# A hand-set order for the turn from the first FFN to the dilated attention

## The chip, the core and the metric

The kernel runs on one core of a Trainium2 chip. The metric is the device time of one execution in microseconds (us). Most of the work is fp32 matrix products on TensorE. Each fp32 operand is split into a high part and a low part, and a product is made of three matmuls: high by high, high by low, low by high.

## The reference

A block of two layers works on 512 tokens of 1024 features. Layer 0 has an HGRN2 mixer and a SwiGLU FFN, layer 1 a dilated attention of three groups and a second FFN. The change lies between the first FFN and the attention:

```python
def rms_norm(x, g):
    xf = x.astype(jnp.float32)
    y = xf * lax.rsqrt(jnp.mean(xf * xf, axis=-1, keepdims=True) + NORM_EPS)
    return (y * g.astype(jnp.float32)).astype(x.dtype)
...
    proj = (u @ w_in).astype(jnp.float32).reshape(B, S, N_GROUPS, 3, ATT_HEADS, ATT_HEAD_DIM)
    for gi, (window, dilation) in enumerate(DILATED_GROUPS):
        q = apply_partial_rope(proj[:, :, gi, 0], cos, sin) * scale
        k = apply_partial_rope(proj[:, :, gi, 1], cos, sin)
        v = proj[:, :, gi, 2]
...
        y = swiglu_ffn(u, ffn_w_in[layer], ffn_w_out[layer])
        h = h + (1.0 + g2) * rms_norm(y, norm_g[layer, 3])
```

So the turn takes the FFN's output y, adds its normalized and gated form to h, normalizes the new h into u, and multiplies u by the attention's weights. The values of the first group (eight heads, 1024 columns) come first, in two halves of 512 columns.

## The kernel before

**Tiles.** The 512 tokens are four tiles of 128 (t = 0 to 3), the 1024 features eight tiles of 128 (kt = 0 to 7). uh and ul hold the high and the low part of u with the features on the partitions. A value product of one half for one token tile is 8 x 3 = 24 matmuls of 512 columns in one PSUM bank (`three`, L582 to L584), with weights in two tiles: kt 0 to 3 and kt 4 to 7.

**The turn, step by step** (class `Turn`, L603 on). For each token tile: squares of y (`sq_y`, ScalarE, L618), gating (`gated`, VectorE, L627), a reciprocal root (`r_y`, VectorE L631 and GpSimd L633), the update of h (`upd`, VectorE, L643), squares of h (`sq_h`, ScalarE), a root again (`r_h`), the normalized row xn (VectorE, L657), eight transposes on TensorE into two banks (`flip`, L663), scale and shift into u (`u_of`: four steps on ScalarE, L673, and four on VectorE, L675), the high parts (`hi_of`, ScalarE, L678) and the low parts (`lo_of`, GpSimd, L682).

**Weights.** A `Stream` loads weights in a fixed sequence through two raw buffers on the SP queue (L67 to L76). `process_to` splits a whole tile of 2048 columns: high part on ScalarE (L96), low part on VectorE (L97). `pieces` does the same in two halves that the caller places (L116, L117). There are three buffers of high and low parts: the fourth value tile needs the buffer of the first, which the first half's products of all token tiles must have read. The sequence here is: first half, kt 0 to 3 and 4 to 7; second half, kt 0 to 3 and 4 to 7; the first query-key tile; then quarters for the next query-key pair and half tiles for further values.

**What sets the order.** Inside `with tc.manual_schedule(engines=ORDERED)` each of TensorE, ScalarE, VectorE and GpSimd keeps the order of the program text. Outside, the framework's scheduler chooses the order; it may also put such instructions between those of a hand-set stretch. The end of the first FFN (L1126 to L1185) is hand-set. It holds the value products of the first half (`v_prod`, copied out at L1675) and, among them, the transposes of token tiles 2 and 3; a half split of the third weight tile and four DMAs that store h (L1183) come behind these.

Then follows, left to the scheduler: the rearranged copies of uh and ul called `apart` (eight each on ScalarE, L1700, and VectorE, L1701), the products of the second half with `tok_proj` (L1480, copied out at L1683, stored at L1685), `token_sums` (four sums, L875, and four differences, L876 to L879, on VectorE; then four high parts over uh, ScalarE L883, and four low parts over ul, VectorE L884), and the masks (GpSimd L1707 to L1712, VectorE L1713 to L1716).

**The plan.** The rest of the attention is placed by `Plan`, which gives every task an engine, a cost and a due time and writes out one hand-set order. It begins with the first query-key tile (48 matmuls with `apart`, L1822). Next is a query-key pair made with seven products instead of eight: its weights are split and summed at L1868 to L1894, and its products use the parts from `token_sums`. Behind it come value units, whose weights are split at L2002 and L2003 and summed at L2007.

Of the kernel before, what the change touches and what calls it, by code (L numbers as in the profile page):

```python
# [11 lines left out]
F32 = mybir.dt.float32  # L12
# [5 lines left out]
P = 128  # L18
S = 512
D = 1024  # L20
KT = D // P
NT = S // P
# [5 lines left out]
ORDERED = {mybir.EngineType.PE, mybir.EngineType.Activation, mybir.EngineType.DVE, mybir.EngineType.Pool}  # L28
# [9 lines left out]
SEEN = lambda t: t.rearrange("p (x n a) -> p x a n", a=2, n=P)  # L38
PLACED = lambda t: t.rearrange("p (x a n) -> p x a n", a=2, n=P)
# [259 lines left out]
def block_kernel(tc, x, c, positions, ada_w, ada_b, norm_g, hgrn_w_in, lower, hgrn_norm_g, hgrn_w_out,  # L299
                 attn_w_in, attn_w_out, ffn_w_in, ffn_w_out, inv_freq, out):  # L300
    nc = tc.nc
    act, dve, pool, pe = nc.scalar, nc.vector, nc.gpsimd, nc.tensor
    x2, out2 = x[0], out[0]
    V4 = lambda t: t.rearrange("p (a b) -> p a b", a=4)
    L4 = lambda a: a.rearrange("p (l r) -> p r l", r=4)
    R4 = lambda a: a.rearrange("p (r l) -> p l r", r=4)

    with ExitStack() as ctx:
# [7 lines left out]
        def bank(tag):  # L316
            uid[0] += 1
            return psum.tile([P, 512], F32, name=f"ps_{tag}{uid[0]}", tag=tag, bufs={"mm": 4, "a": 2, "b": 2}[tag])
# [19 lines left out]
        h = base.tile([P, NT, D], F32, name="h")  # L338
# [183 lines left out]
        def av(g, hf):  # L522
            return [wtok(AW, kq, (g * 3 + 2) * D + hf * 512) for kq in range(2)]
# [9 lines left out]
        def values(hf, gs):  # L533

            for g in gs:
                order.append(("v", g, hf))
                at.extend([("half", w[1]) for w in av(g, hf)])
# [29 lines left out]
        st = Stream(nc, wp, items, 2, 3)  # L567
# [5 lines left out]
        uh = base.tile([P, KT, S], F32R, name="uh")  # L573
        ul = base.tile([P, KT, S], F32R, name="ul")
# [5 lines left out]
        def three(ps, ah, al, bh, bl, start, stop, part=False):  # L580
            ps, bh, bl = LAID(ps), TAKE(bh), TAKE(bl)
            pe.matmul(ps, ah, bh, start=start, stop=False, skip_group_check=part)  # L582
            pe.matmul(ps, ah, bl, start=False, stop=False, skip_group_check=part)  # L583
            pe.matmul(ps, al, bh, start=False, stop=stop, skip_group_check=part)  # L584
# [436 lines left out]
        def ffn(l, first, close, nxt, side):  # L1021
            turns.close()
            close()
            with ExitStack() as fx:
# [4 lines left out]
                with ExitStack() as qx:  # L1029
# [6 lines left out]
                    for j in range(PLAIN[l]):  # L1036
                        if j == 0:
                            pss = first
                        else:
                            pss = []  # L1040
                            for i in range(2):
                                w = st.take()
# [33 lines left out]
                for j in range(NJ - 2):  # L1076
# [3 lines left out]
                    w = st.take()  # L1080
# [5 lines left out]
                ws = [st.take(), st.take(1)]  # L1086
# [39 lines left out]
                with tc.manual_schedule(engines=ORDERED):  # L1126
                    mm(0)
                    y_steps(0)
                    n.upds(0)
                    n.r_h(0)  # L1130
                    n.xn(0)
                    mm(1)
                    y_steps(1)
                    n.upds(1)
                    mm(2, (0, 1))
                    n.flip(0, [bank("mm"), bank("a")])
                    n.u_of(0, 0)
                    n.u_of(0, 1)
                    n.r_h(1)
                    n.parts_of(0, 0)  # L1140
                    n.xn(1)
                    n.parts_of(0, 1)
                    mm(3, (0, 1))
                    for hi_f, lo_f in st.pieces(2, True):
                        hi_f()
                        lo_f()
                    st.fill()
                    mm(2, (2, 3))
                    y_steps(2)
                    n.upds(2)  # L1150
                    n.flip(1, [bank("mm"), bank("b")])
                    n.u_of(1, 0)
                    n.u_of(1, 1)
                    n.r_h(2)
                    n.parts_of(1, 0)
                    n.parts_of(1, 1)
                    n.xn(2)
                    mm(3, (2, 3))
                    y_steps(3)
                    fx.close()  # L1160
                    v_prod = nxt[1]()
                    vw = [st.take(0), st.take(0)]
                    v_prod(vw, 0, range(8))
                    n.upds(3)
                    n.flip(2, [bank("mm"), bank("a")])
                    n.r_h(3)
                    n.u_of(2, 0)
                    n.u_of(2, 1)
                    n.parts_of(2, 0)
                    n.parts_of(2, 1)  # L1170
                    n.xn(3)
                    v_prod(vw, 1, range(8))
                    n.flip(3, [bank("mm"), bank("b")])
                    n.u_of(3, 0)
                    n.u_of(3, 1)
                    n.parts_of(3, 0)
                    n.parts_of(3, 1)
                    for hi_f, lo_f in st.pieces(2, True):
                        hi_f()
                        lo_f()  # L1180
                    st.fill()
                    for t in range(NT):
                        act.dma_start(h_away[t], h[:, t])  # L1183
                    v_prod(vw, 2, range(8))
                    v_prod(vw, 3, range(8))  # L1185
                turns.close()


# [288 lines left out]
        head = sc.tile([P, S], F32, name="head")  # L1477
        pool.memset(head, 0.0)

        def tok_proj(done):  # L1480

            ws = [st.take(), st.take(1)]
            for t in range(NT):
                ps = bank("mm")
                tok = slice(t * P, (t + 1) * P)
                for kt in range(KT):
                    whi, wlo = ws[kt // 4]
                    w = slice((kt % 4) * 512, (kt % 4 + 1) * 512)
                    three(ps, uh[:, kt, tok], ul[:, kt, tok], whi[:, w], wlo[:, w], kt == 0, kt == KT - 1)
                done(t, ps)  # L1490

        C16 = lambda a: a.rearrange("p (c t) -> p c t", t=32)
        B44 = lambda a: a.rearrange("p (b c t) -> p b c t", b=4, c=4)

# [117 lines left out]
        for p in range(4):  # L1612
            tiles = []
            whi, wlo = st.take()
            for k in range(2):
                ps = block(whi, wlo, k * P, 256)
# [6 lines left out]
            whi, wlo = st.take()  # L1623
            for k in range(2):
                ps = block(whi, wlo, k * P, 256)
# [4 lines left out]
                if k == 1:  # L1630
                    for i in range(2):
                        n = fl.n + i
# [17 lines left out]
        oT, V, store = [], [], []  # L1650
        scr = dpool.tile([NH, 2, S, 2], F32, name="scr")
        h_away = dpool.tile([NT, P, D], F32, name="h_away")
        back = lambda t: lambda: act.dma_start(h[:, t], h_away[t])
        heads = {}
        def open_attention():

            ctx.enter_context(hx)
            otp = hx.enter_context(tc.tile_pool(name="a_ot", bufs=1))
            oT.extend(heads_of(otp))
            store.append(otp)  # L1660
            hx.enter_context(cx)
            vp = cx.enter_context(tc.tile_pool(name="a_v", bufs=1))
            V.extend(vp.tile([P, NT, 512], F32, name=f"V{g}") for g in range(3))
            banks = {}

            def v_prod(ws, t, kts):
                if t not in banks:
                    banks[t] = bank("mm")
                tok = slice(t * P, (t + 1) * P)
                for kt in kts:  # L1670
                    w = slice((kt % 4) * 512, (kt % 4 + 1) * 512)
                    three(banks[t], uh[:, kt, tok], ul[:, kt, tok], ws[kt // 4][0][:, w], ws[kt // 4][1][:, w],
                          kt == 0, kt == KT - 1)
                if kts[-1] == KT - 1:
                    act.copy(PLACED(V[0][:, t]), SEEN(banks[t]))  # L1675
            return v_prod

        ffn(0, first, h0.close, ((1, 0), open_attention), "right")
        v_away = dpool.tile([P, NT, 512], F32, name="v_away")

        def to_away(t, ps):

            act.copy(PLACED(V[1][:, t]), SEEN(ps))  # L1683
            if t == NT - 1:
                act.dma_start(v_away, V[1])  # L1685

        PNs, PR_h = [h[:, k].rearrange("p (t n) -> p t n", t=4) for k in range(2)], h[:, 2].rearrange("p (t n) -> p t n", t=4)
        flip_no = [0, 0]
# [7 lines left out]
        up = upx.enter_context(tc.tile_pool(name="a_u", bufs=1))  # L1696
        up.tile([P, 64], F32, name="pad")
        apart = [up.tile([P, KT, S], F32R, name=f"apart{k}") for k in range(2)]
        for kt in range(KT):
            act.copy(V4(apart[0][:, kt]), L4(uh[:, kt]).bitcast(F32))  # L1700
            dve.tensor_copy(V4(apart[1][:, kt]), L4(ul[:, kt]).bitcast(F32))  # L1701
        tok_proj(to_away)
        th, tl = (t.rearrange("p (a b) n -> p a (b n)", a=4).rearrange("p a (b n) -> p a b n", b=4) for t in (uh, ul))

        token_sums(th, tl, h.rearrange("p t (a n) -> p (t a) n", a=2), *apart)()
# [8 lines left out]
        dve.tensor_copy(lqf, lq)  # L1714
        dve.tensor_scalar(lqf, lqf, 0.5, NEG, op0=OP.is_ge, op1=OP.mult)
        dve.tensor_tensor(maskR[:, P:256], maskR[:, 0:P], lqf, op=OP.min)  # L1716

        plan = Plan()
        ticks, clock = Fillers(), [0.0]
# [534 lines left out]
        rows_of, ws, opened = [], [], ("opened", 0)  # L2254
# [104 lines left out]
```

## Time and profile before

| | us |
|---|---|
| median of three runs | 1475.56 |
| lowest and highest | 1474.87, 1476.01 |
| profiled execution | 1476.0 |
| its span in the trace | 1474.1 |
| TensorE, VectorE, ScalarE, GpSimd busy | 1430.7, 1113.8, 824.7, 190.1 |

The stretch that the change touches runs from about 650 to 702 us of the span. In a time line each row is: start, duration, engine, line, operation, out<-in, shapes, count. In square brackets stands the idle time of the engine before it and what ended that. PE is TensorE, DVE VectorE, ACT ScalarE, POOL GpSimd. SPq and ACTq are the queues that issue DMAs. A row with a count holds several instructions in a row, and its duration is theirs together.

### The profile page before, as it was taken

The numbers are of one execution on the slowest core, as the hardware profiler recorded it, in microseconds if no ns is written. First come the engines' busy times: TensorE is split into PE (matmuls) and PEld (weight loads), VectorE is DVE, ScalarE is ACT, GpSimd is POOL, SyncE is SP. The second block draws the span as 40 slices with busy tenths as digits, with TensorE's granted clock in tenths as the row PEclk, the third lists the DMA queues.
The fourth block names the chain that finished last, engine by engine and source line by source line (L and its number), as shares of the span: only waits on it lengthen the run. The fifth ranks groups of instructions, "written<-read, shape, count | busy, mean of one in ns | idle before, by whom it ended". The sixth has DMA issues, their size and how long they took to land. (4 is left out here: it accounts for less than half of the span.)

```text
span 1474.1 us, 25335 instructions
## 1 busy us (share of the span) xinstructions
PE 1430.7 (97%) x9903; PEld 1312.5 (89%) x9903; DVE 1113.8 (76%) x1800; ACT 824.7 (56%) x1484; POOL 190.1 (13%) x173
## 2 busy tenths in 40 slices
PE   8999999999999999998999999999999999999998
PEld 6777888889999987787998999999998999999887
DVE  4588688488888876777788877788776978887644
ACT  4434442474555542267748778657896645555332
POOL 1011102031111100231000110001012211110100
PEclk9999999999999999999999999999999999999999
DMA  9656554223333355734244543254344233334541
GB/s 308 192 192 197 172 173 145 84 78 94 110 109 111 108 178 195 230 113 143 90 122 119 147 123 109 64 172 137 94 138 149 86 104 112 110 110 149 191 143 58
DMA packets 212872, 201.10 MB, mean 136 GB/s; under 512 B 8920, under 2 KB 170640, under 8 KB 212496
## 3 DMA queue, kind: packets, MB, share of 16 engines
q1 hardware_dynamic: 209776, 192.71, 42.3%
q10 hardware_dynamic: 1952, 6.65, 1.2%
q8 instruction: 78, 1.28, 0.4%
q0 software_dynamic: 1024, 0.12, 0.2%
q14 instruction: 42, 0.34, 0.1%
HBM read 192.30 MB, written 5.30 MB: 134 GB/s over the span
## 5 line engine op out<-in xcount | busy, mean ns | idle before, releaser
L96 ACT CAST hi<-raw 128x2048 fp32r<-128x2048 f32 x41 | 78.1, 1904 | 140.7 <-DMA raw<-in_ffn_w_out_dram 82.5
L1822 PE MATMUL ps_mm<-apart,hiq 128*128 128x256 f32 (+1 forms) x608 | 137.4, 320 | 3.5 <-ACT xs L1936 2.8
L97 DVE TENSOR_TENSOR lo<-raw,hi 128x2048 fp32r<-128x2048 f32 x41 | 98.0, 2393 | 55.7 <-ACT hi L96 55.6
L582 PE MATMUL ps_mm<-uh,hi 128*128 128x512 f32 (+1 forms) x368 | 130.7, 355 | 0.0
L583 PE MATMUL ps_mm<-ul,hi 128*128 128x512 f32 (+1 forms) x368 | 128.4, 349 | 1.6 <-DVE ul L682 1.6
L584 PE MATMUL ps_mm<-uh,lo 128*128 128x512 f32 (+1 forms) x368 | 128.3, 349 | 0.0
L1822 PEld LDWEIGHTS ps_mm<-apart,hiq 128*128 128x128 f32 x608 | 99.9, 191 | 9.8 <-ACT xs L1936 3.4
L954 DVE TENSOR_TENSOR loq<-raw,hiq 128x1024 fp32r<-128x1024 f32 x72 | 85.0, 1221 | 20.2 <-ACT hiq L950 20.2
L963 PE MATMUL ps_mm<-th,hiq 128*128 128x256 f32 x360 | 99.0, 275 | 0.0
L963 PE MATMUL ps_mm<-tl,hiq 128*128 128x256 f32 x360 | 99.0, 275 | 0.0
L963 PE MATMUL ps_mm<-th,loq 128*128 128x256 f32 x360 | 99.0, 275 | 0.0
L1822 PE MATMUL ps_mm<-apart,loq 128*128 128x256 f32 (+1 forms) x304 | 95.4, 314 | 0.6 <-DVE loq L1958 0.6
L934 POOL TENSOR_TENSOR raw<-raw 128x512 f32<-128x512 f32 x36 | 47.7, 1326 | 320.1 <-DVE spare L930 165.3
L583 PE MATMUL ps_mm<-lo,oh 128*128 128x512 f32 x208 | 80.0, 385 | 5.5 <-DVE lo L97 5.4
L950 ACT CAST hiq<-raw 128x1024 fp32r<-128x1024 f32 x72 | 72.2, 1049 | 21.1 <-DVE raw L938 16.5
L582 PEld LDWEIGHTS ps_mm<-uh,hi 128*128 128x128 f32 x368 | 69.9, 190 | 12.4 <-issue 5.3
L582 PE MATMUL ps_mm<-hi,oh 128*128 128x512 f32 x208 | 79.6, 383 | 0.8 <-ACT hi L96 0.8
L583 PEld LDWEIGHTS ps_mm<-ul,hi 128*128 128x128 f32 x368 | 70.1, 190 | 9.3 <-DVE ul L682 2.0
L584 PEld LDWEIGHTS ps_mm<-uh,lo 128*128 128x128 f32 x368 | 70.0, 190 | 6.9
L1822 PE MATMUL ps_mm<-uh,hiq 128*128 128x256 f32 x256 | 72.0, 281 | 0.2 <-ACT ps_mm L1911 0.2
L1822 PE MATMUL ps_mm<-ul,hiq 128*128 128x256 f32 x256 | 71.2, 278 | 0.0
L1822 PE MATMUL ps_mm<-uh,loq 128*128 128x256 f32 x256 | 71.1, 278 | 0.0
(478 smaller groups left out, 4739.0 us busy)
## 6 DMA issues: line engine op xcount, KB each, us to landing
raw<-in_ada_w_dram SPq DMA_DIRECT2D x40, 1024.0 KB, 5.2
raw<-in_ffn_w_in_dram SPq DMA_DIRECT2D x144, 256.0 KB, 4.0
raw<-in_ffn_w_out_dram SPq DMA_DIRECT2D x22, 1024.0 KB, 4.9
raw<-in_attn_w_in_dram SPq DMA_DIRECT2D x64, 256.0 KB, 4.5
raw<-in_hgrn_w_in_dram SPq DMA_DIRECT2D x12, 1024.0 KB, 5.4
raw<-in_attn_w_in_dram SPq DMA_DIRECT2D x12, 1024.0 KB, 5.1
raw<-in_ffn_w_in_dram SPq DMA_DIRECT2D x8, 1024.0 KB, 5.0
raw<-in_attn_w_in_dram SPq DMA_DIRECT2D x16, 512.0 KB, 5.1
```

The lines of the kernel that those rows point to most:

```text
L96: self.nc.scalar.copy(hi, t)
L97: self.nc.vector.tensor_sub(lo, t, hi.bitcast(F32))
L582: pe.matmul(ps, ah, bh, start=start, stop=False, skip_group_check=part)
L583: pe.matmul(ps, ah, bl, start=False, stop=False, skip_group_check=part)
L584: pe.matmul(ps, al, bh, start=False, stop=stop, skip_group_check=part)
L934: pool.tensor_add(r[:, 2], r[:, 2], r[:, 0])
L950: act.copy(hi, src)
L954: dve.tensor_sub(lo, src, hi.bitcast(F32))
L963: pe.matmul(LAID(ps), w[x][:, a], TAKE(us[kt][y]), start=begin and kt + m == 0, stop=kt == 3 and m == 2, skip_group_check=True)
L1822: pe.matmul(LAID(dst()), x, TAKE(y), start=begin and i == 0, stop=i == len(todo) - 1, skip_group_check=True)
```

## The change

The two halves of the value work are put into one hand order. The split of the second half's first weight tile (`hi_a`, `lo_a`, `hi_b`, `lo_b`) moves ahead of and between the transposes of token tile 2. Half of token tile 1's products moves ahead of those transposes. Two portions of the second half, kt 0 to 3 of token tiles 0 and 1, run in banks "a" and "b" on either side of the transposes of tile 3. The split of the second half's second weight tile moves into the hand-set stretch. What follows, up to the masks, gets a hand-set order of its own: two `apart` copies of each kind ahead of each token tile's remaining products, the first query-key tile's split ahead of tile 1's.

```diff
                     v_prod(vw, 0, range(8))
                     n.upds(3)
+                    (hi_a, lo_a), (hi_b, lo_b) = st.pieces(2, True)
+                    hi_a()
+                    n.r_h(3)
+                    lo_a()
+                    hi_b()
+                    v_prod(vw, 1, range(4))
                     n.flip(2, [bank("mm"), bank("a")])
-                    n.r_h(3)
                     n.u_of(2, 0)
                     n.u_of(2, 1)
+                    n.xn(3)
+                    lo_b()
                     n.parts_of(2, 0)
                     n.parts_of(2, 1)
-                    n.xn(3)
-                    v_prod(vw, 1, range(8))
+                    st.fill()
+                    v_prod(vw, 1, range(4, 8))
+                    vn.append(st.take(0))
+                    v_next(0, range(4))
                     n.flip(3, [bank("mm"), bank("b")])
                     n.u_of(3, 0)
                     n.u_of(3, 1)
                     n.parts_of(3, 0)
                     n.parts_of(3, 1)
+                    v_next(1, range(4))
+                    for t in range(NT):
+                        act.dma_start(h_away[t], h[:, t])
+                    v_prod(vw, 2, range(8))
+                    v_prod(vw, 3, range(4))
                     for hi_f, lo_f in st.pieces(2, True):
                         hi_f()
                         lo_f()
                     st.fill()
-                    for t in range(NT):
-                        act.dma_start(h_away[t], h[:, t])
-                    v_prod(vw, 2, range(8))
-                    v_prod(vw, 3, range(8))
+                    v_prod(vw, 3, range(4, 8))
...
+            def v_next(t, kts):
+                if (1, t) not in banks:
+                    banks[1, t] = bank("abmm"[t] if t < 2 else "mm")
+                values(V[1], v_tiles, banks[1, t], t, kts)
...
-        for kt in range(KT):
-            act.copy(V4(apart[0][:, kt]), L4(uh[:, kt]).bitcast(F32))
-            dve.tensor_copy(V4(apart[1][:, kt]), L4(ul[:, kt]).bitcast(F32))
-        tok_proj(to_away)
+        order_of_steps = ctx.enter_context(ExitStack())
+        order_of_steps.enter_context(tc.manual_schedule(engines=ORDERED))
+        v_tiles.append(st.take(0))
+        for t in range(NT):
+            for kt in (2 * t, 2 * t + 1):
+                act.copy(V4(apart[0][:, kt]), L4(uh[:, kt]).bitcast(F32))
+                dve.tensor_copy(V4(apart[1][:, kt]), L4(ul[:, kt]).bitcast(F32))
+            if t == 1:
+                st.process_to(st.done + 1)
+            v_steps[0](t, range(4 if t < 2 else 0, KT))
+        act.dma_start(v_away, V[1])
...
         dve.tensor_tensor(maskR[:, P:256], maskR[:, 0:P], lqf, op=OP.min)
+        order_of_steps.close()
```

`values` is the old body of `v_prod` with the destination, the weights and the bank as arguments; it copies the bank out after kt 7. `v_steps[0]` is `v_next`. The number of matmuls, copies, splits and bytes is the same.

More of the change, by code (lines that the diff above doesn't have):

```diff
@@ L1160, in ffn @@
                     fx.close()
-                    v_prod = nxt[1]()
+                    v_prod, v_next, vn = nxt[1]()
                     vw = [st.take(0), st.take(0)]
@@ L1478, in block_kernel @@
         pool.memset(head, 0.0)
[L1480 to L1485, printed above, removed]
-                for kt in range(KT):
[L1487 to L1490, printed above, removed]
         C16 = lambda a: a.rearrange("p (c t) -> p c t", t=32)
@@ L1664, in open_attention, with values @@
             banks = {}
-            def v_prod(ws, t, kts):
-                if t not in banks:
-                    banks[t] = bank("mm")
+            def values(dst, ws, b, t, kts):
                 tok = slice(t * P, (t + 1) * P)
@@ L1671, in v_prod @@
                     w = slice((kt % 4) * 512, (kt % 4 + 1) * 512)
-                    three(banks[t], uh[:, kt, tok], ul[:, kt, tok], ws[kt // 4][0][:, w], ws[kt // 4][1][:, w],
-                          kt == 0, kt == KT - 1)
+                    three(b, uh[:, kt, tok], ul[:, kt, tok], ws[kt // 4][0][:, w], ws[kt // 4][1][:, w], kt == 0, kt == KT - 1)
                 if kts[-1] == KT - 1:
-                    act.copy(PLACED(V[0][:, t]), SEEN(banks[t]))
-            return v_prod
+                    act.copy(PLACED(dst[:, t]), SEEN(b))
+            def v_prod(ws, t, kts):
+                if (0, t) not in banks:
+                    banks[0, t] = bank("mm")
+                values(V[0], ws, banks[0, t], t, kts)
+            def v_next(t, kts):
+                if (1, t) not in banks:
+                    banks[1, t] = bank("abmm"[t] if t < 2 else "mm")
+                values(V[1], v_tiles, banks[1, t], t, kts)
+            v_steps.append(v_next)
+            return v_prod, v_next, v_tiles
+        v_tiles, v_steps = [], []
         ffn(0, first, h0.close, ((1, 0), open_attention), "right")
         v_away = dpool.tile([P, NT, 512], F32, name="v_away")
[L1681 to L1685, printed above, removed]
         PNs, PR_h = [h[:, k].rearrange("p (t n) -> p t n", t=4) for k in range(2)], h[:, 2].rearrange("p (t n) -> p t n", t=4)
@@ L1698, in block_kernel @@
         apart = [up.tile([P, KT, S], F32R, name=f"apart{k}") for k in range(2)]
-        for kt in range(KT):
-            act.copy(V4(apart[0][:, kt]), L4(uh[:, kt]).bitcast(F32))
-            dve.tensor_copy(V4(apart[1][:, kt]), L4(ul[:, kt]).bitcast(F32))
-        tok_proj(to_away)
+        order_of_steps = ctx.enter_context(ExitStack())
[9 more added lines that the diff above has]
+        act.dma_start(v_away, V[1])
         th, tl = (t.rearrange("p (a b) n -> p a (b n)", a=4).rearrange("p a (b n) -> p a b n", b=4) for t in (uh, ul))
```

## The prediction

> **What bounds the kernel now.** I read the page's first part, then the time line of each engine around the turn, then the waits and busy time behind it. The page and a table of two stretches:
>
> ```profile
> span 1474.1 us, 25335 instructions
> PE 1430.7 (97%) x9903; PEld 1312.5 (89%) x9903; DVE 1113.8 (76%) x1800; ACT 824.7 (56%) x1484; POOL 190.1 (13%) x173
> ```
> ```profile
> core 0: us, PE busy (x) PEld busy (x) DVE busy (x) ACT busy (x) POOL busy (x), PEclk, DMA share, GB/s
> 650.31:701.66 51.35, 45.54 (x210) 38.90 (x209) 38.75 (x54) 36.14 (x53) 11.58 (x15) 0.97 0.38 123
> 720.71:752.79 32.08, 30.40 (x262) 29.86 (x262) 29.87 (x41) 21.97 (x29) 1.65 (x2) 1.00 0.22 71
> ```
>
> TensorE has 97% overall, but the first stretch, which holds all value products of the turn, leaves it idle for 5.8 us. In the other, some twenty microseconds on, VectorE is busy for 29.87 of 32.08 us, as much as TensorE. So two engines take turns as the bound, and a gain on one must be followed to the other. TensorE's own time line:
>
> ```profile
> 650.31 0.38 PE L582 MATMUL ps_mm<-hi,uh 128*128 128x512 f32 x1
> ...
> 656.90 0.63 PE L663 MATMUL ps_mm<-ident,xn 128*128 128x128 f32 x4 [1.25 <-DVE xn L657]
> ...
> 664.32 0.63 PE L663 MATMUL ps_mm<-ident,xn 128*128 128x128 f32 x4 [1.16 <-DVE xn L657]
> ...
> 683.89 0.55 PE L582 MATMUL ps_mm<-hi,uh 128*128 128x512 f32 x1 [3.40 <-ACT hi L96]
> 684.24 0.63 PE L583 MATMUL ps_mm<-lo,uh 128*128 128x512 f32 x1
> ...
> 687.63 0.38 PE L584 MATMUL ps_mm<-hi,ul 128*128 128x512 f32 x1
> ...
> 701.66 0.59 PE L1822 MATMUL ps_mm<-apart,hi 128*128 128x512 f32 x2
> ...
> 712.02 0.38 PE L1822 MATMUL ps_mm<-apart,hiq 128*128 128x256 f32 x2
> ```
>
> From 701.66 to 712.02 lie the 48 products of the first query-key pair: 0.216 us each, 2.59 for twelve, 5.18 for twenty-four. The three gaps make 5.8 us. After the third the matmuls take 0.63 instead of 0.38 us until 687.63; 9 of them need 3.74 us instead of 1.94, another 1.8. So 7.6 us can at most be won here. Why the third gap:
>
> ```profile
> 669.84 11.72 ACT L1700 CAST apart<-uh 128x512 fp32r<-128x512 f32 x8 [0.22 <-POOL ul L682]
> 681.47 0.57 ACT L1675 COPY V<-ps_mm 128x512 f32<-128x512 f32 x1
> 681.95 1.89 ACT L96 CAST hi<-raw 128x2048 fp32r<-128x2048 f32 x1
> ```
>
> Eight rearranging copies of 1.465 us hold ScalarE, and the value copy and the last weight split wait behind them. They are outside a hand-set stretch, and the scheduler put them ahead of a copy inside one: a hand-set order binds its own instructions only.
>
> **TensorE after the change, by queues.** The products of token tile 0 start at 650.31 as before and end at 655.49. Now twelve products of tile 1 stand ahead of the transposes:
>
> ```profile
> 656.00 1.14 ACT L678 CAST uh<-u 128x512 fp32r<-128x512 f32 x2
> ...
> 661.80 0.19 ACT L618 ACTIVATION_READ_ACCUMULATOR junk<-h 128x1 f32 x1
> ```
> ```profile
> 656.70 2.52 POOL L682 TENSOR_TENSOR ul<-u,uh 128x512 fp32r<-128x512 f32 x2 [0.76 <-ACT uh L678]
> ```
> ```profile
> L117 DVE TENSOR_TENSOR lo<-raw,hi 128x1024 fp32r<-128x1024 f32 x4 | 6.6, 1696 | 3.5 <-ACT hi L116 3.5
> ...
> L657 DVE TENSOR_SCALAR xn<-h,rr 128x1024 f32<-128x1024 f32 x4 | 3.0, 750 | 1.3 <-POOL rr L633 1.3
> L675 DVE TENSOR_SCALAR u<-ps_b,cols 128x128 f32<-128x128 f32 x8 | 2.7, 400 | 1.3 <-PE ps_b L663 1.3
> ...
> L1873 DVE TENSOR_TENSOR raw<-raw 128x512 f32<-128x512 f32 x4 | 2.7, 690 | 0.1
> L1894 DVE TENSOR_TENSOR loq<-raw,hiq 128x1024 fp32r<-128x1024 f32 x2 | 2.4, 1222 | 1.1 <-ACT hiq L1893 1.1
> L1869 DVE TENSOR_TENSOR loq<-raw,hiq 128x512 fp32r<-128x512 f32 x3 | 2.1, 687 | 0.1
> ...
> L1716 DVE TENSOR_TENSOR maskR<-maskR,V 128x128 f32<-128x128 f32 x1 | 0.3, 291 | 0.1
> ```
> ```profile
> L116 ACT CAST hi<-raw 128x1024 fp32r<-128x1024 f32 x4 | 4.0, 1042 | 0.0
> ```
>
> They need the first uh piece (656.6) and, from the third matmul on, the first ul piece of GpSimd (656.70 + 1.26 = 658.0): two stalls of about 1.0 us, end at 660.2. Eight transposes, about 0.85 (an estimate from the 0.63 of four, pipelined), then twelve products, to 663.65. The first portion of the new half follows. Its weight split begins when ScalarE has the last square (662.0): high piece to 663.0, low piece on VectorE to 664.25, a stall of 0.4. The second low piece is queued behind four u steps (1.4) and xn (0.75), so it starts at 666.4. GpSimd's ul pair of tile 2 runs then. Rows of one shape give 1.22 us without GpSimd and 1.70 as the mean beside it; I take 1.70, since the overlap is full: 668.1, a stall of 2.4. The Trainium skill, SBUF — State Buffer, section SBUF: two separate sides, speaks against this placing: a VectorE instruction with two SBUF inputs and a GpSimd one that reads SBUF exclude each other for a whole instruction. By that rule the piece would start only after GpSimd's, end some 0.8 us later than by my row, and the sum would be 0.8 worse.
>
> From 669.1: transposes (670.0), second portion (672.5), tile 2 of the first half (677.7), tile 3 in two parts (680.3, 682.9). The last weight split has its buffer at 680.3, and its pieces, 1.04 on ScalarE and 1.22 on VectorE each, stay just ahead. Then twelve, twelve, twenty-four, twenty-four: 685.5, 688.1, 693.3, 698.5. Stalls of 4.8 instead of 7.6, and the first query-key pair starts 3.2 us earlier than at 701.66.
>
> **What the new order does to ScalarE and VectorE.** The rows of before:
>
> ```profile
> 671.94 6.62 DVE L1701 CAST apart<-ul 128x512 fp32r<-128x512 f32 x8
> 678.29 2.53 DVE L875 TENSOR_TENSOR h<-apart,apart 128x1024 f32<-128x1024 f32 x2
> ...
> 685.01 4.49 DVE L97 TENSOR_TENSOR lo<-raw,hi 128x2048 fp32r<-128x2048 f32 x2
> ...
> 700.17 1.23 DVE L884 TENSOR_TENSOR ul<-h,uh 128x1024 fp32r<-128x1024 f32 x1 [5.88 <-ACT uh L883]
> ...
> 703.66 1.22 DVE L884 TENSOR_TENSOR ul<-h,uh 128x1024 fp32r<-128x1024 f32 x1
> ...
> 710.56 1.22 DVE L1894 TENSOR_TENSOR loq<-raw,hiq 128x1024 fp32r<-128x1024 f32 x1 [1.11 <-ACT hiq L1893]
> ```
>
> Before, VectorE starts the token sums at 678.29 and has the last of their low parts at 704.9. Afterwards two of the eight rearrangements stand ahead of each tile's value copy. On ScalarE the copy of tile 0 waits for TensorE at 685.5, and queued behind it are rearrangements 3 and 4 (2 x 1.465) and the 1.89 us split of the first query-key weights: 685.7 + 0.57 + 2.93 + 1.89 = 691.1. On VectorE everything else is queued behind the low part of that split, although half of it could run: an idle stretch from 684.2 to 691.1. Then: low part 2.25, four rearrangements 3.3, four sums of 1.22, four differences of 1.22, four low parts of 1.17 (their spacing with the pipeline's overlap), to 711.0. The masks, run in a pause before, add 0.9 (four small steps, the largest 0.29). The last token low part is 6.1 us later than before.
>
> What follows on VectorE is the plan's own preparation: three L1869, four L1873, two L1894, 7.2 us by their group rows, 7.1 with the overlap. It ends before at 711.78, afterwards at 719.0 in whatever order these mix, 7.2 later; waits on ScalarE (the 1.11 above) may add 1. The other bound: were the plan's steps taken first, L1894 would end at 713.5, and the token parts TensorE needs 1.3 us into its next unit at 718, where it had them at 713.35 (712.02 + 1.33); the delay is then 4.8 on TensorE itself. TensorE, at 708.9 there, waits for VectorE either way. The 3.2 us are lost within ten.
>
> How long the lateness lives is read from the next rows. The last L1894 frees the raw buffer whose next load, landing, split and use follow:
>
> ```profile
> 711.81 0.37 SPq L76 DMA_DIRECT2D raw<-in_attn_w_in_dram  x1
> ```
> ```profile
> raw<-in_attn_w_in_dram SPq DMA_DIRECT2D x1, 1024.0 KB, 5.1
> ```
> ```profile
> 719.02 1.36 ACT L2002 CAST hiq<-raw 128x1024 fp32r<-128x1024 f32 x1
> ```
> ```profile
> 720.41 1.29 DVE L2003 TENSOR_TENSOR loq<-raw,hiq 128x1024 fp32r<-128x1024 f32 x1 [3.55 <-ACT hiq L2002]
> 722.42 1.23 DVE L2007 TENSOR_TENSOR raw<-raw,raw 128x1024 f32<-128x1024 f32 x1 [0.72 <-ACT hiq L2002]
> ...
> 739.34 1.35 DVE L2003 TENSOR_TENSOR loq<-raw,hiq 128x1024 fp32r<-128x1024 f32 x1 [1.04 <-ACT hiq L2002]
> ```
> ```profile
> 748.91 0.38 PE L1822 MATMUL ps_mm<-loq,apart 128*128 128x256 f32 x1 [0.85 <-DVE loq L2003]
> ```
>
> Afterwards: 719.0 + 5.1 = 724.1, split to 725.5, low part from 725.6 instead of 720.41: 5.2 late, 2 us being taken up by ScalarE, which was busy until 719.02. Between there and 748.91, where TensorE already waits for VectorE, the rows show pauses of 0.72 and 1.04. I let half of these absorb: 4.3 us late at a place with no slack. Nothing after it runs ahead of TensorE by more, so the delay stays.
>
> **Edits without a price.** The four stores of h (each 0.5 MB) go to ScalarE's queue before the last value copies; the sums that overwrite h start after 696, over 20 us later; without that cover the sums wait one landing, about the 5.1 us of the load above. The load of the first query-key weights is issued earlier, the one of the first half-weights later (693.4 for some 689.5); its use lies beyond 713, so it is hidden, else it costs its 5 us. On the SP queue nothing else is passed. GpSimd has only the masks behind its ul pairs. Two portions accumulate in banks "a" and "b", next used by the plan's scores after 720.
>
> **The sum.** The profiled execution took 1476.0 us with a span of 1474.1; the median is 1475.56. TensorE's own gain of 3.2 is not added: the place that decides is VectorE's, 4.3 later than before. 1475.56 + 4.3 = 1479.9. From 1.5 (half of the lateness absorbed before 748) to 7.5 (ScalarE waits, a slow stretch after a new gap): 1477.0 to 1483.1.
>
> **Rivals.** 1. The lateness is absorbed: the 3.55, 0.72 and 1.04 us pauses, and a plan whose TensorE steps tolerate a late token part, take all of it, and the TensorE gain is lost at 748.91, where it already waited. 1475.6, within 1.5. For it: 5.3 us of pauses; against: 7.2 are needed. 2. TensorE decides alone: the 3.2 us stay won, or 4.8 if the split pieces wait less, 1470.8 to 1472.4. It decides if the token sums end before about 707, for which the low part of the query-key split must start before 687; ScalarE's rows speak against that. The Trainium skill, Perfetto Trace Analysis, section Optimization Strategies, would have it so: keep TensorE as busy as possible and start what it waits for sooner. The page's 97% agrees with that reading, the stretch with VectorE at 29.87 of 32.08 does not. 3. Slower still: the stall ahead of the token products is over 3.4 us, and the matmuls behind it run at 0.63 again, 1.8 us, with ScalarE's waits on top; above 1483. It decides if TensorE rather than VectorE comes last at 748. 4. The order is not what the text says: since stretches bind only themselves, the scheduler may weave the second differently into the first; worth either sign, and counted half to 1 and half to 2.
>
> **Chances.** Forecast 0.50, rival 1 0.25, rival 2 0.19, rival 3 0.06. A measurement of this kernel can tell 0.2%, 2.95 us: of the forecast about a fifth lies below 1478.5. Faster 0.18, same 0.37, slower 0.45. The range goes from 1472.0, in rival 2, to 1483.0.
>
> **What would show it.** Right: no 3.4 us gap at 684 and value products that end near 698; VectorE idle between 684 and 691; the last L884-type step near 711; a TensorE wait of 3 us or more on the token parts or the first loq near 709; the 1 MB load of 711.81 near 719; the wait at 749 some 4 us later. Wrong: token sums done by 707, or a TensorE time line at 749 that is earlier than before.

## The result, and the profile after

The changed kernel takes 1481.01 us (median of 5 runs, 1480.53 to 1481.74), the kernel before 1475.87 in its runs beside it (1474.87 to 1478.42). The ratio is 1.0034, with a 95% interval from 1.0019 to 1.0049: slower by 2.8 to 7.2 us. The forecast was 1479.9. The profiled execution of after took 1480.53 us.

The lines of the page and of the table by stretches that answer to those of before (columns as there; the third row, the time at half clock, overlaps the second and reaches 2 us past it):

```profile
span 1478.7 us, 25330 instructions
PE 1434.0 (97%) x9903; PEld 1315.7 (89%) x9903; DVE 1111.3 (75%) x1801; ACT 824.6 (56%) x1485; POOL 192.0 (13%) x173
```
```profile
650.31:701.66 51.35, 48.32 (x229) 41.17 (x228) 31.07 (x46) 35.15 (x53) 12.80 (x15) 1.00 0.42 142
701.66:720.71 19.05, 13.97 (x69) 12.47 (x68) 18.02 (x27) 10.80 (x17) 0.00 (x0) 0.79 0.12 34
712.50:722.70 10.20, 7.48 (x33) 7.19 (x34) 7.18 (x15) 6.32 (x12) 0.00 (x0) 0.50 0.32 103
```

In the first stretch TensorE is busier than before (48.32 us for 45.54), so the change does there what it says. In the next 19 us it is idle for 5 us and has a granted clock of 0.79, while VectorE is busy for 18.02 of 19.05: work that was VectorE's in the first stretch (31.07 us now, 38.75 before) has moved here. TensorE's own time line:

```profile
656.73 0.48 PE L582 MATMUL ps_mm<-hi,uh 128*128 128x512 f32 x1 [0.77 <-ACT uh L678]
...
658.08 0.48 PE L584 MATMUL ps_mm<-hi,ul 128*128 128x512 f32 x1 [0.66 <-POOL ul L682]
...
667.35 0.48 PE L583 MATMUL ps_a<-lo,uh 128*128 128x512 f32 x1 [1.51 <-DVE lo L117]
...
697.90 0.59 PE L1832 MATMUL ps_mm<-apart,hi 128*128 128x512 f32 x2
...
713.85 0.58 PE L1832 MATMUL ps_mm<-ul,hiq 128*128 128x256 f32 x1 [3.16 <-DVE ul L884]
...
717.93 0.58 PE L1832 MATMUL ps_mm<-uh,hiq 128*128 128x256 f32 x1 [1.37 <-ACT ps_mm L1921]
...
753.44 0.38 PE L1832 MATMUL ps_mm<-loq,apart 128*128 128x256 f32 x1 [0.50 <-DVE loq L2013]
```

The gap of 3.40 us at 684 is gone, and the first query-key products start at 697.90 instead of 701.66. Then TensorE stands 3.16 us for the low token part and 1.37 us for ScalarE, and at the loq wait of 748.91 (loq is the low part of a split piece of weights) it is 4.5 us late. VectorE's time line says why:

```profile
690.50 2.29 DVE L97 TENSOR_TENSOR lo<-raw,hi 128x2048 fp32r<-128x2048 f32 x1 [7.09 <-ACT hi L96]
692.71 3.32 DVE L1707 CAST apart<-ul 128x512 fp32r<-128x512 f32 x4
695.96 4.61 DVE L875 TENSOR_TENSOR h<-apart,apart 128x1024 f32<-128x1024 f32 x4
...
709.18 4.61 DVE L884 TENSOR_TENSOR ul<-h,uh 128x1024 fp32r<-128x1024 f32 x4
...
716.38 1.22 DVE L1904 TENSOR_TENSOR loq<-raw,hiq 128x1024 fp32r<-128x1024 f32 x1 [0.65 <-ACT hiq L1903]
...
724.82 1.34 DVE L2013 TENSOR_TENSOR loq<-raw,hiq 128x1024 fp32r<-128x1024 f32 x1 [4.34 <-ACT hiq L2012]
```

It stands 7.09 us for the query-key split, with four rearrangements behind it, and so begins the token sums at 695.96; before, at 678.29. The last low part ends at 713.8 (704.9 before), the last loq of the first pair begins at 716.38 (710.56), the split of the next load at 724.82 (720.41).

**How the runs are compared.** The runs of one kernel differ by some us, and the traces differ in short stretches of half clock that come in one and not in another, several of them ahead of the change (near 246, 571 and 634 us, where the programs don't differ). So beside the medians, each trace is measured from a place of its own, the last pair of L643 on VectorE ahead of the turn. That row before and after:

```profile
659.76 1.41 DVE L643 SCALAR_TENSOR_TENSOR h<-yg,rr,h 128x512 f32<-128x512 f32 x2 [0.59 <-POOL rr L633]
```
```profile
659.80 1.42 DVE L643 SCALAR_TENSOR_TENSOR h<-yg,rr,h 128x512 f32<-128x512 f32 x2 [0.58 <-POOL rr L633]
```

From it to the first query-key product (the row with ps_mm<-apart,hi), and to the loq wait of 748.91 in before: 41.90 and 89.15 us before, 38.10 and 93.64 after. So TensorE enters the query-key products 3.8 us early and passes the loq wait 4.5 us late. All kernels in this measure ("start" and "loq wait" against before; the ratio is to the runs of before on the same chip, with 12 runs of each kernel, but 5 of the first and 9 of the sixth):

| kernel | start, us | loq wait, us | median, us | ratio, 95% |
|---|---|---|---|---|
| after | -3.8 | +4.5 | 1481.01 | 1.0034, 1.0019 to 1.0049 |
| slow clock filled | -3.8 | +4.3 | 1479.07 | 1.0017, 1.0001 to 1.0032 |
| first stretch alone | -0.8 | -0.7 | 1476.54 | 0.9999, 0.9982 to 1.0016 |
| second stretch alone | -5.4 | +1.3 | 1477.52 | 1.0013, 1.0000 to 1.0025 |
| split earlier | -3.8 | +3.3 | 1478.17 | 1.0012, 0.9996 to 1.0028 |
| parts in order of use | -3.8 | +4.7 | 1482.35 | 1.0044, 1.0029 to 1.0060 |
| token sums ahead | -2.3 | -1.2 | 1476.79 | 0.9993, 0.9976 to 1.0009 |
| the same, VectorE delayed | -2.3 | +2.8 | 1480.14 | 1.0027, 1.0016 to 1.0038 |
| the same, chain shorter | -2.3 | -1.4 | 1476.93 | 1.0005, 0.9994 to 1.0017 |
| second alone, sums ahead | -5.4 | -3.8 | 1472.76 | 0.9975, 0.9963 to 0.9987 |

The start column hardly says what the ratio will be; the loq column does, to within some 2 us. Neither counts what comes behind 749 us: six of the eleven traces, before and after among them, have a stretch of half clock between 1020 and 1035 us, and from the loq wait to the end they take 725.2 to 727.2 us, the five others 723.4 to 724.8. Before stands at 1477.54 us in the chip's runs beside the second, third, fifth and seventh kernel, at 1475.53 beside the fourth, sixth, eighth and ninth, at 1476.73 beside the last.

### The profile page after: what moved, and what is told of

Read it like the earlier page. It is cut to its first block, busy times and chain, and to the rows that moved or that the text cites. A ratio compares the mean times of both kernels' runs of the same rounds, so it can differ in the third digit from the quotient of the medians.

```text
span 1478.7 us, 25330 instructions
## 1 busy us (share of the span) xinstructions
PE 1434.0 (97%) x9903; PEld 1315.7 (89%) x9903; DVE 1111.3 (75%) x1801; ACT 824.6 (56%) x1485; POOL 192.0 (13%) x173
```

## The experiments

Theory A is the prediction's: VectorE's chain from the rearrangements over the token sums to the last loq is late, and TensorE waits for it at 749 us, whatever it won before. Theory B is the third rival grown large: the new gap and the slow clock behind it are the loss. Theory C: the interleaving between the transposes costs.

**The slow clock filled.** 32 needless matmuls of 128x256 into the bank of the first token products, which start it anew afterwards, keep TensorE busy through the gap.

```diff
+                for x, y in fill() if fill else ():
+                    pe.matmul(LAID(dst()), x, TAKE(y), start=True, stop=True, skip_group_check=True)
...
-                run(both, 0, 1, T3, True)
+                run(both, 0, 1, T3, True, 32 if hd == 0 and g == 1 else 0)
```

> The changed kernel with 32 needless matmuls put ahead of the first products that use the token parts, in a bank that these then overwrite: TensorE works through its 3.2 us gap (710.3 to 713.9), and the matmuls behind it should run at full speed instead of some 9 us at half. Theory A (VectorE's work is late, and TensorE is held by it some 40 us on, whatever its clock did): the time stays at about 1480.7, less than 0.5 us off, with a TensorE wait for a loq near 749 that is longer. Theory B (the gap and the slow clock behind it are the loss): about 2 us or more come back, 1478.8 or below.

The wait for the low part shrinks from 3.16 us to 0.40, but the next, for ScalarE's copy, grows from 1.37 to 2.59, with 3.4 us of half clock behind it:

```profile
PE ps_mm L1834 <- ACT ps_mm L1924: 2.6, 1, 2.6
PE ps_mm L1834 <- DVE ul L884: 0.4, 1, 0.4
```

At the loq wait TensorE is 4.3 us late, 0.2 less than after. Where a gap is taken away without making VectorE faster, TensorE waits a little further on. The median is lower than that of after by more than this: by the ratios it is 2.5 us above before and after is 5.0, but their intervals overlap (0.1 to 4.7 and 2.8 to 7.2 us). The trace shows 0.2 us of it up to the loq wait and 1.6 behind it, where this trace lacks the stretch of half clock past 1020 us; so I go by the trace and call the median unclear here.

**The first stretch alone.** The second stretch without its hand-set order.

```diff
-        order_of_steps.enter_context(tc.manual_schedule(engines=ORDERED))
```

> The changed kernel without the hand-set order behind the first FFN: value portions and splits between the transposes stay, the rearrangements, token sums and masks are left to the scheduler. Theory A (the second hand-set stretch makes the token sums late): the token low parts end near 705 again, and the loss goes, 1475 to 1477, though TensorE gets a gap of 3 to 5 us near 683 back, as eight rearrangements stand ahead of the last weight split on ScalarE. Theory C (the interleaving between the transposes is what costs): it stays near 1480.

The loss is gone, and the gain too: 0.8 us ahead at the start, 0.7 at the loq wait, 0.9999. TensorE's gap behind the rearrangements is back, with 2.13 us, less than the 3 to 5 expected. Theory C falls, since all the interleaving between the transposes is still there.

**The second stretch alone.** The opposite: everything between the transposes as before, the second half's products all behind them.

```diff
-                    (hi_a, lo_a), (hi_b, lo_b) = st.pieces(2, True)
...
-                    v_next(0, range(4))
...
-        v_tiles.append(st.take(0))
+        v_tiles.extend([st.take(0), st.take(0)])
...
-            v_steps[0](t, range(4 if t < 2 else 0, KT))
+            v_steps[0](t, range(KT))
```

> The first stretch, between the transposes, as before the change, the hand-set order only from the rearrangements to the masks. Theory A (VectorE's token sums come late because the hand-set order puts them behind the split and the rearrangements): the query-key split no longer waits for the second value half's products to be pulled ahead, so the last low token part is about 3 us earlier than after the change, and TensorE at 750 us runs 1 to 2 us behind the kernel before: 1476.5 to 1479.0 us. Theory B (the wait on the token parts near 710 us and the slow clock behind it are the loss): TensorE reaches that place some 3 us later than after the change, for the value products are not pulled forward, so the wait is short, the clock stays up, and the time is that of before, 1475 to 1476.5. Theory C (the interleaving between the transposes costs): without it all the loss goes, 1475 to 1476.

```profile
695.28 0.59 PE L1821 MATMUL ps_mm<-apart,hi 128*128 128x512 f32 x2
```
```profile
749.15 0.38 PE L1821 MATMUL ps_mm<-loq,apart 128*128 128x256 f32 x1 [0.54 <-DVE loq L2002]
```

This is the plainest evidence. Its L643 row stands at 658.74, so the first query-key product comes 36.54 us behind it, 5.4 us earlier than before (41.90) and even 1.6 earlier than after: the second order alone removes the 3.4 us gap and its slow clock, since ScalarE's copies no longer stand ahead of the last value split, and the products between the transposes cost TensorE 1.6 us. And with 5.4 us in hand it passes the loq wait 1.3 us late (90.41 for 89.15). Theory A held in time and place. B expected a short wait and a clock that stays up; it had waits of 2.2 and 2.6 us and a slow clock, and lost far less than after. What had changed was VectorE's chain: its token sums begin 31.82 us behind the L643 row (690.56), 4.3 sooner than in after (36.16).

**The split earlier.** The query-key split one tile earlier in the hand-set order.

```diff
-            if t == 1:
+            if t == 0:
                 st.process_to(st.done + 1)
```

> The changed kernel with one step moved: the split of the first query-key weights stands ahead of token tile 0's products instead of tile 1's, so its low part can start on VectorE at about 685 and not at 690.5. Theory A as the prediction put it (what is queued behind this split makes the token sums late): 4 us come back, about 1477. Theory A with another gate (the last two rearrangements on ScalarE, queued behind tile 2's value copy and done at 697.3): the last two sums can't start before 697.3 either, against 698.3 now, so only about 1 us comes back, 1480.

```profile
685.13 2.29 DVE L97 TENSOR_TENSOR lo<-raw,hi 128x2048 fp32r<-128x2048 f32 x1 [1.58 <-ACT hi L96]
...
692.07 2.49 DVE L875 TENSOR_TENSOR h<-apart,apart 128x1024 f32<-128x1024 f32 x2
696.61 2.36 DVE L875 TENSOR_TENSOR h<-apart,apart 128x1024 f32<-128x1024 f32 x2 [2.06 <-ACT apart L1706]
```

The split now starts before the 687 that the prediction named, the 7.09 us are 1.58, and yet only 1.2 of the 4.5 us come back at the loq wait (by the ratios more, 1.0012 for 1.0034, with intervals that overlap). There is a second gate: the last two token sums need all rearrangements, and ScalarE makes its last two behind the value copy of tile 2 (693.06), which waits for TensorE.

**The parts in the order of their use.** TensorE needs part 1 first, and it is cut last.

```diff
-                for k in (3, 0, 2, 1):
+                for k in (1, 3, 0, 2):
```

> The kernel after, with the token sums cut into parts in the order of their use (1, 3, 0, 2) and not 3, 0, 2, 1: the first part that TensorE needs is ready some 3 us earlier, and VectorE has as much to do as before. Theory A: the wait of 3.16 us for the low part goes and with it, perhaps, the slow clock, but the last pieces of query and key weights still leave VectorE at 716 to 718 us, so TensorE only waits there: at 750 us it is within 1 us of the kernel after, 1480 to 1481.5 us. Theory B: 3 us of wait and some 4 us of slow clock come back, at 750 us it is 3 to 5 us earlier, 1476 to 1478.

The wait for the low part is gone altogether. In its place (TensorE, then ScalarE):

```profile
719.37 0.58 PE L1832 MATMUL ps_mm<-uh,hiq 128*128 128x256 f32 x1 [6.78 <-ACT ps_mm L1921]
```
```profile
716.74 1.04 ACT L1903 CAST hiq<-raw 128x1024 fp32r<-128x1024 f32 x1 [3.73 <-DVE raw L1883]
...
718.96 0.36 ACT L1921 COPY ps_mm<-ps_mm 128x256 f32<-128x256 f32 x1
```

One wait of 6.78 us for two of 3.16 and 1.37. The copy L1921 that TensorE waits for is queued on ScalarE behind the cast of L1903, and that waits for a sum of VectorE's at the end of the late chain. At the loq wait: +4.7 us, as late as after. B expected 3 to 5 us back, and falls here.

**Token sums ahead.** Another hand-set order from the same parts, for which `token_sums` is returned in three pieces (`add`, `differences`, `cut`): all eight low rearrangements first, then four high ones, two sums, the split, the other four, the other sums and the differences, then the value products, and the cutting last.

```diff
+        for kt in range(KT):
+            low(kt)
+        for kt in range(4):
+            high(kt)
+        add(0, 1)
+        st.process_to(st.done + 1)
+        for kt in range(4, KT):
+            high(kt)
+        add(3, 2)
+        differences()
+        for t in range(NT):
+            v_steps[0](t, range(4 if t < 2 else 0, KT))
...
+        cut()
```

> The changed kernel with the second stretch in another hand-set order: four rearrangements on ScalarE, the query-key split, then the other four, all ahead of the value copies; on VectorE all eight rearrangements, two sums, the split, the other sums and the differences; the products as they are; the token parts last. Theory A: VectorE has the differences done by about 698 instead of 708 and the last loq of the first seven products by 711 instead of 717.6, TensorE keeps most of its 3.7 us up to there, and the time is at or below that of the kernel before, 1473.5 to 1476. Theory B without A: the same if the gap near 710 goes. Theory C: not below 1478.

From +4.5 to -1.2 us at the loq wait: 5.7 us by VectorE's and ScalarE's order alone, although TensorE starts the query-key products 1.5 us later than in after (-2.3 for -3.8). The ratio, 0.9993, cannot be told from 1; its interval lies below that of after.

**The same, VectorE delayed.** Four needless steps in front of the cutting.

```diff
+        for k in range(4):
+            part = same[:, 2 * k:2 * k + 2]
+            dve.scalar_tensor_tensor(part, part, 1.0, part, op0=OP.mult, op1=OP.max)
         cut()
```

> The kernel with the token sums pulled ahead, with four needless steps of 128x1024 on VectorE (four times 1.22 us, 4.9 us, each part replaced by the larger of itself and itself, so nothing changes) between the token differences and the token parts. Theory A: VectorE sets the end of this stretch, so most of the 4.9 us comes out at the end: TensorE at 750 us 3.5 to 4.9 us later than without them, 1480 to 1482 us. A rival (the pulled-ahead order gains for another reason, and VectorE has room): under 1.5 us later, 1477 to 1478.

```profile
701.65 4.63 DVE L1731 SCALAR_TENSOR_TENSOR h<-h 128x1024 f32<-128x1024 f32 x4
```

4.63 us put on VectorE come out as 4.0 on TensorE at the loq wait (+2.8 for -1.2) and, by the two ratios, as some 0.0034 of 1476, 5.0 us, of the time. VectorE's chain has hardly any room: by the trace, some 0.9 us on TensorE for each us put on it.

**The same, chain shorter.** Two high rearrangements on VectorE in its wait for ScalarE, masks ahead, parts in the order of use.

```diff
         for kt in range(4, KT):
-            high(kt)
+            if kt < 6:
+                high(kt)
+            else:
+                dve.tensor_copy(V4(apart[0][:, kt]), L4(uh[:, kt]).bitcast(F32))
...
-        cut()
+        cut((1, 3, 0, 2))
```

> The kernel with the token sums pulled ahead, with three things more: VectorE makes the last two of the eight high rearrangements in the 3.57 us in which it waited for ScalarE to make them; the masks stand ahead of the second pair of sums, and not at the end; the parts are cut in the order of their use. Theory A: the sums come 1.9 us earlier and the masks, about 1 us, leave the end of the chain: TensorE at 750 us 2 to 3 us earlier than with the sums pulled ahead alone, 3 to 4 us earlier than before the change: 1472 to 1474.5 us. A rival (TensorE's own work or ScalarE now decides): no more than 1 us is gained on 1476.8, the time is within 0.2% of the kernel before.

A miss: 0.2 us instead of 2 to 3. VectorE has its differences done 1.0 us sooner (37.4 us behind the L643 row, for 38.4 with the sums ahead alone), but the last low token part ends 49.0 us behind that row in both:

```profile
704.88 1.23 DVE L1921 TENSOR_TENSOR loq<-raw,hiq 128x1024 fp32r<-128x1024 f32 x1 [2.08 <-ACT hiq L1920]
...
708.97 3.49 DVE L887 TENSOR_TENSOR ul<-h,uh 128x1024 fp32r<-128x1024 f32 x3
```

VectorE waits 2.08 us for a weight part that ScalarE casts (L1920) behind the last value copy, and that copy, at 703.32, waits for TensorE's products. So the bound leads back to TensorE, as the rival said, and the next gain had to come from its start.

**The second stretch alone, sums ahead.** This takes TensorE's best start (-5.4) and the short chain together; the masks stand ahead of the second pair of sums.

```diff
+        for kt in range(KT):
+            low(kt)
+        for kt in range(4):
+            high(kt)
+        v_steps[0](0, range(KT))
+        add(0, 1)
+        st.process_to(st.done + 1)
...
+        for kt in (4, 5):
+            high(kt)
+        v_steps[0](1, range(KT))
+        for kt in (6, 7):
+            high(kt)
+        add(3, 2)
+        differences()
...
+        cut((1, 3, 0, 2))
```

> The first stretch as before the change, and behind it one hand-set order with the token sums pulled ahead: the split of the second value half, all eight low rearrangements, the first sums, the query-key split, the masks, the other sums, the differences, and the value products in between; parts cut in the order of use. With the second stretch alone TensorE began the query-key products 5.4 us earlier than before, and still was 1.3 us late at 749 us because of VectorE. Theory A: here VectorE has its differences done some 3 us sooner and the masks, 1 us, are off the end of its chain, so TensorE at 749 us is 2 to 4 us ahead of the kernel before: 1471.5 to 1473.5 us against 1475.5. A rival (the plan behind is bound by TensorE's and ScalarE's own steps whatever VectorE does, as the last kernel with sums ahead suggests): no more than 1.4 us ahead, 1474 us or later.

```profile
697.45 0.59 PE L1839 MATMUL ps_mm<-apart,hi 128*128 128x512 f32 x2
```
```profile
699.89 1.22 DVE L1911 TENSOR_TENSOR loq<-raw,hiq 128x1024 fp32r<-128x1024 f32 x1
...
703.97 3.49 DVE L887 TENSOR_TENSOR ul<-h,uh 128x1024 fp32r<-128x1024 f32 x3
```
```profile
746.30 0.38 PE L1839 MATMUL ps_mm<-loq,apart 128*128 128x256 f32 x1 [1.00 <-DVE loq L2020]
```
```profile
701.66:720.71 19.05, 17.39 (x122) 16.10 (x121) 13.48 (x18) 15.94 (x26) 0.00 (x0) 1.00 0.26 91
```

Its L643 row stands at 660.91. The start is 5.4 us early, 3.8 of them are left at the loq wait, and the time is 0.9975 of before (0.9963 to 0.9987): faster than both kernels. The last value copy comes at 697.65, VectorE no longer waits behind it, and the last low token part ends 46.6 us behind the L643 row, 2.4 sooner than in the kernel with the shorter chain; the loq wait gains the same 2.4 us (-3.8 for -1.4). In the 19 us in which after left TensorE idle for 5 us, it is busy for 17.39 at full clock.

## Why the prediction was right

- **The forecast case.** Right in sign, size and mechanism, the size in part by luck, as the end of the chain shows below: 4.3 us late at the loq wait was forecast, 4.5 is measured; 1479.9 us, and 1481.01 is the median. The first rival let the pauses take all the lateness up. They take 1.4 us of it (5.8 late at the last loq of the pair, 716.38 for 710.56; 4.4 at 724.82 for 720.41). The second, that TensorE decides, has its proof to the contrary in the second stretch alone: 5.4 us in hand, and 1.3 late. The fourth, that the scheduler weaves the stretches, came in part: four of the second stretch's rearrangements run on VectorE at 674.01, ahead of the first stretch's last split (681.05). It did not decide: ScalarE's part of that split began at 679.97, when TensorE released its buffer, for 680.3 in the forecast.
- **TensorE's gain.** 3.2 us were forecast, 3.8 came. The first three stalls came nearly with their size: the twelve products of tile 1 behind the transposes end within 0.2 us of the 663.65, and the third stall ends at 664.28 for 664.25. The second low piece came 0.75 us sooner than forecast (matmul at 667.35 for 668.1), and this is nearly all of the difference. It began 0.3 us sooner (666.08 for 666.4), and I had taken 1.70 us for it, the mean beside GpSimd. The rows of after (VectorE, then GpSimd):

```profile
666.08 1.22 DVE L117 TENSOR_TENSOR lo<-raw,hi 128x1024 fp32r<-128x1024 f32 x1
```
```profile
666.05 3.61 POOL L682 TENSOR_TENSOR ul<-u,uh 128x512 fp32r<-128x512 f32 x2 [3.14 <-ACT uh L678]
```

  VectorE ran at its full speed, and GpSimd's pair took 3.61 us where that of before took 2.52: 1.09 longer, about one VectorE instruction. In before it was VectorE that paid: its two pieces at 668.71, behind GpSimd's pair (667.28, 2.52 us), took 3.31 us together, and two such took 2.36 in after at 681.05, where GpSimd is idle. By the Trainium skill, SBUF — State Buffer, section SBUF: two separate sides, the two exclude each other for a whole instruction, and whichever starts first has the port. The trace agrees with the exclusion, and the rows of before with the order of starting; in after the two records start 0.03 us apart, GpSimd's first, and do not show which had the port. I had let VectorE pay, and here GpSimd did, off the path.
- **VectorE's idle stretch.** Forecast from 684.2 to 691.1; measured, 7.09 us that end at 690.50. The condition beside it ("before 687") was only half of the truth: with the split at 685.13, 1.2 us came back. The step that the prediction lacked is the wait of the last sums for ScalarE's last rearrangements.
- **The end of the chain.** The last low part was forecast for 711.0 and came at 713.8, the last loq for 719.0 and came at 717.6 (716.38 + 1.22). The plan's steps were taken partly ahead of the low parts, the case that the text left open with "in whatever order these mix". The sum was 1.4 us too long: 7.2 late forecast, 5.8 measured. The load went out at 717.63 instead of 719.0, and its loq began at 724.82 instead of 725.6; that the pauses behind it took 0.9 us was too much, the lateness went from 4.4 to 4.5. The two errors nearly cancel, and to that extent it is luck that the forecast came within 0.2 us at the loq wait.
- **The wait of 3 us or more near 709.** It came, 3.16 us that end at 713.85. The slow clock of the third rival came with it, and longer than the 1.8 us there. The rival set the point rightly: it decides only if TensorE comes last at 748, and VectorE did. The kernels with the slow clock filled and with the parts in the order of use show that what TensorE loses there it would else have waited a little further on.
- **Edits without a price.** No row of after that was read around the turn waits for the four stores of h, nor for the half-weights that were loaded later.

Not tried: the first stretch's order without the extra split pieces that it needs, so the 1.6 us that the products between the transposes cost TensorE are not divided between the split's stall (1.51) and the rest.

## What to carry to other kernels

A gap on the busiest engine is worth filling only as far as the next engine's chain lets it run on: follow the gain to the first place where the busiest engine already waits for another, and ask what the change does to that other engine's chain. In a hand-set order every wait stops all that is queued behind it, so a step that waits for a late operand (here a weight split) belongs behind the steps that another engine's path needs (here the rearrangements and token sums). The whole change lost 4.5 us at the loq wait; its second half alone lost 1.3, and won 3.8 once the token sums stood ahead in it.

## What was not expected of the hardware

TensorE's granted clock stays low for long when waits lie close together. In after it is 0.50 from 712.5 to 722.7, 10.2 us, with 33 matmuls in it; the wait before the restart was 3.16 us, and another of 1.37 us fell in the middle. After the one wait of 6.78 us in the kernel with the parts in order it was as long:

```profile
714.60:724.80 10.20, 5.43 (x25) 5.43 (x26) 6.52 (x14) 6.97 (x13) 0.00 (x0) 0.50 0.32 103
```

There work went on at 719.37, so the clock came back after 5.4 us of unbroken work; in after, 4.8 us behind the last wait (717.93). In the kernel with the needless matmuls, 3.4 us of half clock followed a wait of 2.59. The Trainium skill, TensorE: Matmul & The Clock Gate, section What's actually happening, has windows of 3.4 us that run on by themselves, and full rate only after a busy one. The 10.2 us are three such windows and the 3.4 one, so the trace agrees with their length, and with the 6.8 us of half clock in the second stretch alone (711.6 to 718.4). If the three windows of after are counted back from 722.7, the wait of 1.37 us lies in the second, and was enough to make it not count as busy. Nor did the clock need a window without work to fall: with the needless matmuls the wait ended at 718.07 and the clock fell at 719.5, in the midst of work.
